# Weight pieces of a two-layer encoder: their high and low parts kept in DRAM after the first use

## The chip, the cores and the metric

The kernel runs on one core of one Trainium2 chip. The metric is device microseconds for one execution. Three runs of the kernel before gave 2173.24, 2174.95 and 2166.95 us; the median is 2173.24 us.

## The reference

Two groups of rows, `prompt` (1024 tokens, "p" below) and `sample` (512 tokens, "s"), go through the same two layers with the same weights. Cut to what matters here:

```
for l in (0, 1):
    h   = rms_norm(x, norm_g[l])
    u   = h @ w_in[l]                    # 1024 -> 15 chunks of 256 columns
    mk, mv = split(rms_norm(mem) @ w_mem_kv[l])
    l = 0: y1 = short_conv(gb, gc, hc);  y2 = window_attention(q, k, v, sink)
    l = 1: y1 = dense_gqa(q, k, v);      y2 = diff_attention(dq, dk, dv)
    ym  = memory_attention(mq, mk, mv)
    x   = x + (concat(y1, y2, ym) * silu(z)) @ w_out[l]     # 1280 -> 1024
```

`trunk(x_prompt, ...)` and `trunk(x_sample, ...)` are both computed, in float32. So every column chunk of `w_in` and `w_out` is needed by p and again by s.

## The kernel before, in words

TensorE multiplies operands of the type fp32r, which hold less than float32. Each float32 operand is therefore split: the high part is a copy rounded to fp32r, the low part is the source minus the high part. A product is three matmuls: high by high, high by low, low by high (`mm_a` lines 309 to 311, `mm_b` lines 323 to 325).

**Weights.** A chunk is 256 columns of a weight matrix. It comes in pieces of [128, 512] float32, 256 KB each: 4 pieces for `w_in` and `w_mem_kv`, 5 for `w_out`. `load_w` (line 204) does for each piece: a DMA of the raw piece into the ring `wraw` (3 slots), the high part by ScalarE into the ring `whi` (7 slots, line 186), the low part by VectorE where the piece's number is even and by GpSimd where it is odd, into the ring `wlo` (7 slots, line 187). A slot of `whi` or `wlo` comes free when the last matmul on the piece that held it is done; a slot of `wraw` when the low part is made. A piece is taken from DRAM and split again whenever its chunk is used: the run has 16 such pieces for `w_mem_kv`, 252 for `w_in` and 120 for `w_out`, 388 in all.

**Stages.** `in_proj` runs the chunks of a layer's input projection, `out_proj` the four chunks of the output projection for 512 tokens. In `out_proj` a chunk is four groups of 30 matmuls (one group for 128 tokens, 5 pieces x 2 halves x 3 matmuls), and two groups share a PSUM tile `po`, of which there are two. Attention (`swa`, `ax`, `diff`, `mem_attn`) is spread between the projections' products. In the profile of before the stages are, in us from the span's start:

| us | stage |
|---|---|
| 0 to 509 | p, layer 0: memory keys, input projection, attention, convolution |
| 509 to 572 | p, layer 0: `out_proj`, first half of the tokens |
| 572 to 632 | p, layer 0: `out_proj`, second half |
| 632 to 1160 | p, layer 1: memory keys, most of the input projection, attention |
| 1160 to 1506 | s, layer 0: input projection with p's last attention, and one chunk of p again |
| 1506 to 1599 | s, layer 0: `out_proj` |
| 1599 to 1940 | rest of p's layer 1 input projection, s layer 1 input projection, attention |
| 1940 to 2023, 2023 to 2104 | p, layer 1: `out_proj`, first and second half |
| 2104 to 2162 | s, layer 1: `out_proj` |

**Order of the work.** All data DMAs are issued by SyncE (SP) in one queue, in order (`dma`, line 105): a DMA whose operand isn't ready holds up those behind it. The program is written as a sequence, and a scheduler then places every instruction on its engine by a model of when its operands will be there; on an engine the placed order is fixed. `in_order` (line 46) makes the tiles of a ring take its slots in the order of the program. A DMA also waits for the one eight places back in the queue whose completion semaphore it shares.

Of the kernel before, what the change touches and what calls it, by code (L numbers as in the profile page):

```python
# [11 lines left out]
F32R = mybir.dt.float32r  # L12
# [6 lines left out]
D = 1024  # L19
KT = D // 128  # L20
HD = 64
# [24 lines left out]
def in_order(tc, chains):  # L46
    """Slots of a ring go to its tiles in the order of the program: the first writer of each tile is
    scheduled after that of the tile before it."""
    first = {}
    for n, ins in enumerate(tc.nc.cur_bb.bb.instructions):  # L50
        for o in ins.outs:
            t = getattr(o, "bass_ap", None)
            nm = t.tensor.name if t is not None else None
            if nm is not None and nm not in first:
                first[nm] = n, ins
    for tiles in chains.values():
        prev = None
        for _, ins in sorted((first[t.tensor.name] for t in tiles), key=lambda x: x[0]):
            if prev is not None and prev is not ins:
                tc.add_manual_dep(  # L60
                    ins, prev.name,
                    mybir.DependencyInfo(mybir.DependencyClass.NoSync, mybir.DependencyReason.DATA),
                    reason="ring",
                )
            prev = ins
# [3 lines left out]
def trunk_kernel(ctx: ExitStack, tc: tile.TileContext, a: dict, dbg=None):  # L69
# [8 lines left out]
    def ring(pool, shape, dt, tag, nm, stream=""):  # L78
        """a tile of a ring whose slots are taken in the order of the program (of its stream)"""
        t = pool.tile(shape, dt, tag=tag, name=nm, bufs=BUFS[tag])  # L80
        chains.setdefault((tag, stream), []).append(t)
        return t
# [26 lines left out]

    # ------------------------------------------------------------ constants  # L110
    ident_r = const.tile([128, 128], F32R, name="ident_r")
# [35 lines left out]

    # rotary tables with the gains folded in: cos * g and (signed) sin * g of the other half
    tab = {}
# [12 lines left out]

    # ------------------------------------------------------------ scratch in DRAM
    S = {}
# [18 lines left out]

    # ------------------------------------------------------------ helpers
    def split(out_hi, out_lo, src, lo_eng):
# [9 lines left out]
    def first(f):  # L195
        """what feeds the matrix products of the projections goes before the attention's work"""
        return f
        def g(*args, **kw):
            with tc.high_priority():
                return f(*args, **kw)  # L200
        return g

    @first
    def load_w(src, pairs):
        hi, lo = [], []
        for kp in pairs:
            lo_ = ring(sb, [128, 2, 256], F32R, "wlo", "wlo")
            h = ring(sb, [128, 2, 256], F32R, "whi", "whi")
            raw = ring(sb, [128, 2, 256], F32, "wraw", "wraw")
            dma(out=raw, in_=src[kp].rearrange("p (k n) -> p k n", k=2))  # L210
            split(h, lo_, raw, nc.vector if kp % 2 == 0 else nc.gpsimd)
            hi.append(h)
            lo.append(lo_)
        return hi, lo

    def rstd(out, ss, mul, add):
        """out = (ss * mul + add) ** -0.5"""
        n = ss.free_size()
        nc.vector.tensor_scalar(out=ss, in0=ss, scalar1=mul, scalar2=add, op0=ALU.mult, op1=ALU.add)  # L219
        e = mhalf[:, 0:n]  # L220
        if len(ss.shape) == 3:
            e = e.rearrange("p (a b) -> p a b", a=ss.shape[1])
        nc.gpsimd.tensor_tensor(out=out, in0=ss, in1=e, op=ALU.pow)  # L223
# [3 lines left out]
    def bg(n=1):  # L227
        """the next steps of the work that runs between the projections' products"""
        for _ in range(n):
            if BG:  # L230
                with tc.high_priority():
                    BG.pop(0)()

    def norm_steps(rows, put, banks="x"):
        """rms norm of 512 rows (4 sources of [128, D]), transposed; put(t, q, PSUM tile) takes it"""
        hh = {}
# [52 lines left out]
    def load_act(src, pairs):  # L289
        """pairs of [128, 2, 512], hi and lo, of src [128, n, 512] in DRAM"""  # L290
        out = []
# [9 lines left out]
    def mm_a(out, hs, sl, w, mid=None):  # L301
        """out[tok, cols] = act[:, sl].T @ w"""
        whi, wlo = w
# [11 lines left out]
    def mm_b(out, hs, w, csl, mid=None):  # L315
        """out[cols, tok] = w[:, csl].T @ act"""
        whi, wlo = w
# [16 lines left out]
    def stack_now():  # L334
        """the stack of the piece before"""
        while STACK:
            STACK.pop(0)()
# [9 lines left out]
    def between(keep=2):  # L347
        """one step of the work that goes between the projections' products"""
        if len(TAIL) > keep:
# [4 lines left out]
    def store_stack(t, nh, dst, h0, tok):  # L354
        """t [128, 2, nh, 64] (f32, SBUF): hi and lo, transposed, to dst[:, h0:h0+nh, tok:tok+256]"""
        for hp in range(nh // 2):
# [17 lines left out]
    def prep(ps, nh, dst, h0, tok, table=None, gain=None, query=False):  # L374
        """a q or k chunk ps [128, 2, nh, 64] (PSUM): rms norm (and a query's HD ** -0.5), gain, rotation"""
        raw = bw("raw")[:, 0:2 * nh * HD].rearrange("p (t h d) -> p t h d", t=2, h=nh)
# [38 lines left out]
    def put_v(ps, nh, d, dst, t0, tag="stk"):  # L415
        """ps [128, 2, nh, d] (PSUM) to dst[:, 0:nh, t0:t0+2, 0:2d], hi | lo"""
        n = min(nh, 128 // d)
# [9 lines left out]
    def silu2(ps, nm):  # L427
        """2 * silu of ps [128, 512]: ps * (1 + tanh(ps / 2))"""
        th = bw(nm)
# [3 lines left out]

    # ------------------------------------------------------------ input projection
    def rows_of(src, hf=0):
# [8 lines left out]
    def in_proj(g, l, hs, ids, ahead=None, hfs=None):  # L444
        """hfs: the halves of the tokens (all of them if not given)"""
        T = GROUPS[g]
        hfs = range(T // 512) if hfs is None else hfs
        nt = T // 128
        for ci in ids:
            kind, i = CHUNKS[l][ci]  # L450
            if ahead and ci == ids[-1]:
                ahead()
            w = load_w(a["w_in"][l, ci], range(4))
            if kind in ("z", "gch", "gbz"):
# [62 lines left out]
    def conv_cols(g, c, inner):  # L517
        """0.5 * conv along the tokens of inner; the halves follow one another"""
        n = len(inner)
# [23 lines left out]

    # ------------------------------------------------------------ memory keys and values
    def mem_rows():
# [20 lines left out]

    # ------------------------------------------------------------ attention
    def load_q(src, shape):
        """src(rows) -> AP of 64 rows; the hi rows twice and the lo rows twice"""
        out = []  # L570
# [19 lines left out]
    def fold(o, nm):  # L590
        """rows 64..127 of o [128, n] brought to rows 0..63, SBUF"""
        n = o.free_size()
# [4 lines left out]
    def finish_gqa(g, l, o, c0, tok):  # L597
        """o [128, 4, 128]: 4 heads of 128 queries; gated into y's column tiles c0, c0 + 1"""
        zg = aw("zg")[:, 0:256].rearrange("p (c t) -> p c t", c=2)
# [73 lines left out]
    def softmax(s, e, su, nm):  # L673
        """s [128, n, w] (PSUM): nm [128, n] = -max, e [128, n, w] = exp(s + nm), su [128, n] the sums"""
        nc.vector.tensor_reduce(out=nm, in_=s, axis=AXL.X, op=ALU.max, negate=True)  # L675
# [5 lines left out]
    def head_softmax(q2, k, T, e):  # L681
        """one head, 128 queries: e [128, T]: exp(scores - max), with the max of each 512 columns;
        the result [128, T / 512]: what each 512 columns are to be multiplied by"""
        n = T // 512
# [144 lines left out]
    def mem_attn(g, l, half=None, ys=None):  # L829
        """ys: hi and lo of the gated columns, where they stay on chip (512 tokens)"""  # L830
        T = GROUPS[g]
# [44 lines left out]

    # ------------------------------------------------------------ output projection
    Y_ORDER = {("p", 0): (2, 3, 4, 0, 1), ("s", 0): (2, 3, 0, 1, 4), ("p", 1): range(5), ("s", 1): range(5)}
# [4 lines left out]
    def out_proj(g, l, hf, ys, ahead=None):  # L883
# [3 lines left out]
        for ci in range(4):  # L887
            if ahead and ci == 3:
                ahead()
            w = load_w(a["w_out"][l, ci], Y_ORDER[g, l])  # L890
            for tp in range(2):
# [10 lines left out]

    # ------------------------------------------------------------ program
    nxt = {}

    def ahead(key, load):
        """before a phase ends: what it left of the background's work, and the next phase's operands"""
        def f():
# [92 lines left out]

# [1 line left out]
def host_arrays(inputs):  # L1003
# [29 lines left out]
    def pieces(w, idx):  # L1033
        # [K, 256] -> [K / 256, 128, 2 * 256]
        k = w.shape[0]
# [71 lines left out]
```

## Time and profile before

| | |
|---|---|
| median of three runs | 2173.24 us |
| span of the profiled execution, first to last instruction | 2165.8 us |
| TensorE (PE) busy | 2080.9 us, 96% |
| VectorE (DVE), ScalarE (ACT), GpSimd (POOL) busy | 71%, 55%, 50% |
| DMA | 363.74 MB, mean 168 GB/s |

The profile shows no time of its own for the profiled execution beside the span. The median of the runs is 7.4 us above the span, which is what lies around the span together with the spread of the runs (8.0 us from the lowest to the highest). PE is the engine with nearly no idle time, 84.9 us in all. Its busy time is made of overlapping matmuls, so the rate is read from the distance of their starts, not from the length of one. Means by line hide differences between stages, and so the rows below are taken by stage.

### The profile page before, as it was taken

Reading aid. Unit: us, or ns where it says so; the run is one execution under the profiler, and the core shown is the slowest. Engines: PE = TensorE matmul, PEld = TensorE weight load, DVE = VectorE, ACT = ScalarE, POOL = GpSimd, SP = SyncE. Lnnn points to the kernel's source line nnn. Section 1 sums busy time; section 2 is a strip of 40 time slices with the busy share of each in tenths; the row PEclk is TensorE's granted clock in tenths of the full one; section 3 lists DMA queues with packets and bytes.
Section 4 is the critical chain, followed back from the end, with each engine's and each line's share of the span. In section 5 each row is a group of like instructions: output and inputs, shape, how many; then the busy total and the mean of one; then the engine's idle time right before and its main releaser. Section 6 shows DMA issues by size and latency. Waiting matters only on the chain. (4 is left out here: it accounts for less than half of the span.)

```text
span 2165.8 us, 41192 instructions
## 1 busy us (share of the span) xinstructions
PE 2080.9 (96%) x14336; PEld 1916.8 (88%) x14336; DVE 1547.2 (71%) x3264; ACT 1189.7 (55%) x2838; POOL 1075.9 (50%) x1134
## 2 busy tenths in 40 slices
PE   6999999999999999999999989997998999999999
PEld 6988978889999999999998878886997899998999
DVE  8768877745445687877988886777778877875652
ACT  5545633453334566766766655546466666764441
POOL 6845532342225674853855574332346686842331
PEclk9999999999999999999999999998999999999999
DMA  6675463436776522443345565447475566567753
GB/s 229 193 214 169 140 210 106 115 100 212 250 234 220 174 84 88 131 129 114 94 121 180 165 194 166 122 147 229 143 213 179 167 186 203 175 204 217 227 169 105
DMA packets 317408, 363.74 MB, mean 168 GB/s; under 512 B 25360, under 2 KB 222736, under 8 KB 317200
## 3 DMA queue, kind: packets, MB, share of 16 engines
q1 hardware_dynamic: 317200, 361.10, 54.6%
q8 instruction: 114, 1.87, 0.4%
q14 instruction: 94, 0.77, 0.1%
HBM read 261.38 MB, written 99.61 MB: 167 GB/s over the span
## 5 line engine op out<-in xcount | busy, mean ns | idle before, releaser
L187 POOL TENSOR_TENSOR wlo<-wraw,whi 128x512 fp32r<-128x512 f32 x182 | 249.3, 1371 | 322.9 <-ACT whi L186 285.0
L186 ACT CAST whi<-wraw 128x512 fp32r<-128x512 f32 x388 | 237.3, 621 | 254.8 <-PE po L311 74.9
L677 ACT ACTIVATE e<-s,nm 128x512 f32<-128x512 f32 (+1 forms) x416 | 264.4, 640 | 173.4 <-DVE nm L675 124.5
L675 DVE TENSOR_REDUCE nm<-s 128x1 f32<-128x512 f32 (+1 forms) x368 | 248.0, 681 | 37.7 <-PE s L580 36.2
L587 DVE TENSOR_TENSOR ptlo<-pT,pthi 128x512 fp32r<-128x512 f32 x352 | 238.0, 683 | 42.6 <-ACT pthi L586 40.9
L586 ACT CAST pthi<-pT 128x512 fp32r<-128x512 f32 x352 | 201.1, 588 | 118.1 <-PE pT L665 48.4
L309 PE MATMUL po<-whi,ahi 128*128 128x256 f32 x896 | 254.7, 285 | 1.7 <-DVE xr L900 1.4
L310 PE MATMUL po<-wlo,ahi 128*128 128x256 f32 x896 | 254.0, 284 | 0.0
L311 PE MATMUL po<-whi,alo 128*128 128x256 f32 x896 | 253.5, 284 | 0.5 <-DVE alo L187 0.4
L187 DVE TENSOR_TENSOR wlo<-wraw,whi 128x512 fp32r<-128x512 f32 x206 | 175.9, 855 | 105.1 <-ACT whi L186 104.4
L309 PE MATMUL pa<-whi,ahi 128*128 128x256 f32 x768 | 221.2, 288 | 4.0 <-DVE z L431 2.1
L311 PE MATMUL pa<-whi,alo 128*128 128x256 f32 x768 | 221.3, 288 | 0.0
L310 PE MATMUL pa<-wlo,ahi 128*128 128x256 f32 x768 | 221.2, 288 | 0.0
L223 POOL TENSOR_TENSOR rs<-ss,mhalf 128x8 f32<-128x8 f32 (+2 forms) x108 | 141.7, 1313 | 149.7 <-DVE ss L219 141.6
L579 PE MATMUL s<-k,qhh 128*128 128x512 f32 (+2 forms) x512 | 194.6, 385 | 17.2 <-ACT e L677 10.6
L580 PE MATMUL s<-k,qll 128*128 128x512 f32 (+2 forms) x512 | 185.5, 367 | 2.6 <-DMA qll<-st_p1dq 1.6
L309 PEld LDWEIGHTS po<-whi,ahi 128*128 128x128 f32 x896 | 171.1, 191 | 3.7 <-DVE xr L900 1.8
L311 PEld LDWEIGHTS po<-whi,alo 128*128 128x128 f32 x896 | 171.1, 191 | 2.0 <-DVE alo L187 0.9
L310 PEld LDWEIGHTS po<-wlo,ahi 128*128 128x128 f32 x896 | 171.3, 191 | 1.3
L324 PE MATMUL pb<-h,whi 128*128 128x512 f32 x432 | 171.6, 397 | 0.0
L325 PE MATMUL pb<-h,wlo 128*128 128x512 f32 x432 | 171.4, 397 | 0.0
L323 PE MATMUL pb<-h,whi 128*128 128x512 f32 x432 | 170.9, 396 | 0.0
(171 smaller groups left out, 6272.9 us busy)
## 6 DMA issues: line engine op xcount, KB each, us to landing
wraw<-in_w_in_dram SPq DMA_DIRECT2D x252, 256.0 KB, 3.1
wraw<-in_w_out_dram SPq DMA_DIRECT2D x120, 256.0 KB, 3.4
alo<-y_p SPq DMA_DIRECT2D x20, 512.0 KB, 5.0
zg_p<-z SPq DMA_DIRECT2D x32, 256.0 KB, 3.0
k<-st_p1dk SPq DMA_DIRECT2D x14, 512.0 KB, 4.4
v<-dv_p SPq DMA_DIRECT2D x14, 512.0 KB, 5.4
zg<-zg_p SPq DMA_DIRECT2D x48, 128.0 KB, 2.7
y_p<-yo SPq DMA_DIRECT2D x48, 128.0 KB, 2.6
```

Source lines behind the costliest of these rows:

```text
L186: nc.scalar.copy(out=out_hi, in_=src)
L187: lo_eng.tensor_tensor(out=out_lo, in0=src, in1=f32(out_hi), op=ALU.subtract)
L309: nc.tensor.matmul(out=out, lhsT=h, rhs=wh, start=(k == 0), stop=False)
L310: nc.tensor.matmul(out=out, lhsT=h, rhs=wl, start=False, stop=False)
L311: nc.tensor.matmul(out=out, lhsT=l_, rhs=wh, start=False, stop=(k == n - 1))
L324: nc.tensor.matmul(out=out, lhsT=wh, rhs=l_, start=False, stop=False)
L579: nc.tensor.matmul(out=out, lhsT=q2[0], rhs=k, start=True, stop=False)
L580: nc.tensor.matmul(out=out, lhsT=q2[1], rhs=k, start=False, stop=True)
L586: nc.scalar.copy(out=hi, in_=ps)
L587: nc.vector.tensor_tensor(out=lo, in0=ps, in1=f32(hi), op=ALU.subtract)
L675: nc.vector.tensor_reduce(out=nm, in_=s, axis=AXL.X, op=ALU.max, negate=True)
L677: nc.scalar.activation(out=e[:, j, :], in_=s[:, j, :], func=ACTF.Exp, bias=nm[:, j:j + 1], accum_out=su[:, j:j + 1],)
```

## The change

`load_w` gets a key for the chunk. The first time a piece is used, its two parts are stored to two DRAM tiles of 256 KB each after they are made; every later use loads the two parts into `whi` and `wlo` and neither loads the raw piece nor splits. `w_mem_kv`, whose pieces are used once, gets no key.

```diff
-    def load_w(src, pairs):
+    def load_w(src, pairs, key=None):
         hi, lo = [], []
         for kp in pairs:
             lo_ = ring(sb, [128, 2, 256], F32R, "wlo", "wlo")
             h = ring(sb, [128, 2, 256], F32R, "whi", "whi")
+            kept = KEPT.get((key, kp))
+            if kept:
+                dma(out=h, in_=kept[0].rearrange("p (k n) -> p k n", k=2))
+                dma(out=lo_, in_=kept[1].rearrange("p (k n) -> p k n", k=2))
+                hi.append(h)
+                lo.append(lo_)
+                continue
             raw = ring(sb, [128, 2, 256], F32, "wraw", "wraw")
             dma(out=raw, in_=src[kp].rearrange("p (k n) -> p k n", k=2))
             split(h, lo_, raw, nc.vector if kp % 2 == 0 else nc.gpsimd)
+            if key:
+                both = KEPT[key, kp] = [
+                    dr.tile([128, 512], F32R, name=f"w{nm}_{key[0]}{key[1]}_{key[2]}_{kp}") for nm in "hl"
+                ]
+                for x, y in zip(both, (h, lo_)):
+                    dma(out=x.rearrange("p (k n) -> p k n", k=2), in_=y)
             hi.append(h)
             lo.append(lo_)
         return hi, lo
...
-            w = load_w(a["w_in"][l, ci], range(4))
+            w = load_w(a["w_in"][l, ci], range(4), ("i", l, ci))
...
-            w = load_w(a["w_out"][l, ci], Y_ORDER[g, l])
+            w = load_w(a["w_out"][l, ci], Y_ORDER[g, l], ("o", l, ci))
```

The rest of the diff takes out comments and moves line numbers by 16 (lines 309 to 311 become 325 to 327).

The scheduler places the new DMAs among the old ones. On SP, in the first output projection (p, layer 0, first half of the tokens), the queue of before reads as follows. `wraw` is a raw piece, `xr` the residual rows that are loaded, `x_p<-xr` the result that is stored.

```order
L106 DMA x_p<-xr 128x2x256
L106 DMA xr<-in_x_p_dram 128x2x256
L106 DMA wraw<-in_w_out_dram 128x512
L106 DMA xr<-in_x_p_dram 128x2x256
L106 DMA wraw<-in_w_out_dram 128x512
L106 DMA x_p<-xr 128x2x256
L106 DMA wraw<-in_w_out_dram 128x512 x2
```

The same place in the changed kernel; `wh_o_...` and `wl_o_...` are the DRAM tiles of the high and the low part, by chunk and piece:

```order
L106 DMA x_p<-xr 128x2x256
L106 DMA wh_o_2_2_6759<-whi 128x512
L106 DMA xr<-in_x_p_dram 128x2x256
L106 DMA wl_o_2_2_6760<-wlo 128x512
L106 DMA wraw<-in_w_out_dram 128x512
L106 DMA wh_o_2_3_6769<-whi 128x512
L106 DMA wh_o_2_4_6779<-whi 128x512
L106 DMA wl_o_2_3_6770<-wlo 128x512
L106 DMA wl_o_2_4_6780<-wlo 128x512
L106 DMA wraw<-in_w_out_dram 128x512 x2
```

Between the raw pieces stand two stores for each, which wait in the queue for the parts to be made.

On PE, at the change from the third to the last chunk of the last output projection (s, layer 1), the products of before go through one accumulator, `po_28662`, piece by piece (`whi_28639`, `whi_28645`, `whi_28651` are three pieces that follow one another):

```order
L311 MATMUL po_28662<-whi_28639,alo_27971 128x256
L309 MATMUL po_28662<-whi_28645,ahi_27979 128x256
L310 MATMUL po_28662<-wlo_28644,ahi_27979 128x256
L311 MATMUL po_28662<-whi_28645,alo_27978 128x256
L309 MATMUL po_28662<-whi_28645,ahi_27979 128x256
L310 MATMUL po_28662<-wlo_28644,ahi_27979 128x256
L311 MATMUL po_28662<-whi_28645,alo_27978 128x256
L309 MATMUL po_28662<-whi_28651,ahi_27986 128x256
```

In the changed kernel there are two accumulators, `po_28878` and `po_28943`, at that place; `whi_28867` is the third piece of the chunk and `whi_28871` the fourth:

```order
L327 MATMUL po_28878<-whi_28867,alo_28244 128x256
L325 MATMUL po_28943<-whi_28859,ahi_28231 128x256
L326 MATMUL po_28943<-wlo_28858,ahi_28231 128x256
L325 MATMUL po_28878<-whi_28871,ahi_28252 128x256
L327 MATMUL po_28943<-whi_28859,alo_28230 128x256
L325 MATMUL po_28943<-whi_28859,ahi_28231 128x256
L326 MATMUL po_28943<-wlo_28858,ahi_28231 128x256
```

The order now leaves the first accumulator after the third piece, starts the second one on pieces that are there, and comes back to the first as the fourth piece is expected.

On SP at the same place, before, three raw pieces go out together between two results:

```order
L106 DMA xr<-x_s 128x2x256
L106 DMA wraw<-in_w_out_dram 128x512
L106 DMA out_dram<-xr 128x2x256
L106 DMA wraw<-in_w_out_dram 128x512 x3
L106 DMA out_dram<-xr 128x2x256
L106 DMA wraw<-in_w_out_dram 128x512 x2
L106 DMA out_dram<-xr 128x2x256 x4
```

And in the changed kernel:

```order
L106 DMA out_dram<-xr 128x2x256
L106 DMA wlo<-wl_o_3_2_27627 128x512
L106 DMA whi<-wh_o_3_2_27626 128x512
L106 DMA whi<-wh_o_3_3_27636 128x512
L106 DMA wlo<-wl_o_3_3_27637 128x512
L106 DMA whi<-wh_o_3_4_27646 128x512
L106 DMA wlo<-wl_o_3_4_27647 128x512
L106 DMA out_dram<-xr 128x2x256 x3
```

Six loads stand where there were up to three, and each of them needs a slot of `whi` or `wlo` that PE has left, where a raw piece needed only a slot of `wraw`.

## Rows read from the trace of the kernel before

**Rows 1.** The page, part 1: busy time, share of the span, instructions.
```profile
PE 2080.9 (96%) x14336; PEld 1916.8 (88%) x14336; DVE 1547.2 (71%) x3264; ACT 1189.7 (55%) x2838; POOL 1075.9 (50%) x1134
```

**Rows 2.** Waits of PE, whole span: waiter, releaser: us in total, times, longest.
```profile
PE s L579 <- ACT e L677: 10.6, 11, 2.4
...
PE pm L309 <- ACT whi L186: 3.5, 1, 3.5
...
PE pm L310 <- DVE wlo L187: 2.0, 1, 2.0
...
PE pa L310 <- POOL wlo L187: 1.4, 1, 1.4
```

**Rows 3.** The page, part 5: groups, busy us, mean ns of one, idle before.
```profile
L187 POOL TENSOR_TENSOR wlo<-wraw,whi 128x512 fp32r<-128x512 f32 x182 | 249.3, 1371 | 322.9 <-ACT whi L186 285.0
L186 ACT CAST whi<-wraw 128x512 fp32r<-128x512 f32 x388 | 237.3, 621 | 254.8 <-PE po L311 74.9
...
L187 DVE TENSOR_TENSOR wlo<-wraw,whi 128x512 fp32r<-128x512 f32 x206 | 175.9, 855 | 105.1 <-ACT whi L186 104.4
```

**Rows 4.** The page, parts 3 and 6: DMA queue, and issues with us to landing.
```profile
q1 hardware_dynamic: 317200, 361.10, 54.6%
...
wraw<-in_w_in_dram SPq DMA_DIRECT2D x252, 256.0 KB, 3.1
wraw<-in_w_out_dram SPq DMA_DIRECT2D x120, 256.0 KB, 3.4
```

**Rows 5.** Busy time by stage; after the engines PEclk, DMA share, GB/s.
```profile
0.00:509.00 509.00, 480.81 (x2855) 422.89 (x2856) 365.77 (x783) 249.32 (x613) 239.21 (x250) 0.99 0.54 165
509.00:572.00 63.00, 62.62 (x521) 62.34 (x519) 25.36 (x35) 21.50 (x39) 14.93 (x12) 1.00 0.64 210
572.00:632.00 60.00, 57.31 (x479) 56.90 (x477) 26.83 (x41) 18.65 (x33) 11.95 (x10) 1.00 0.77 248
664.00:1160.00 496.00, 492.98 (x3638) 464.93 (x3636) 383.40 (x849) 322.67 (x768) 306.26 (x344) 1.00 0.43 133
1160.00:1470.00 310.00, 297.69 (x1763) 262.26 (x1764) 245.92 (x566) 173.11 (x423) 151.84 (x142) 0.98 0.51 155
1470.00:1506.00 36.00, 25.83 (x122) 19.78 (x121) 24.62 (x60) 21.05 (x67) 9.54 (x19) 0.81 0.89 248
1506.00:1599.00 93.00, 89.93 (x686) 85.15 (x685) 73.56 (x182) 50.73 (x128) 30.05 (x32) 1.00 0.52 153
1599.00:1940.00 341.00, 329.69 (x2318) 303.42 (x2317) 264.81 (x517) 226.54 (x547) 238.28 (x251) 0.98 0.62 188
1940.00:2023.00 83.00, 78.78 (x632) 76.59 (x631) 47.55 (x94) 35.88 (x80) 23.91 (x25) 1.00 0.76 224
2023.00:2104.00 81.00, 78.37 (x635) 76.49 (x634) 47.24 (x81) 40.07 (x94) 26.17 (x33) 1.00 0.65 199
2104.00:2162.00 58.00, 58.00 (x485) 57.79 (x483) 17.17 (x23) 10.87 (x18) 8.26 (x6) 1.00 0.39 119
580.00:600.00 20.00, 18.98 (x161) 18.78 (x160) 11.18 (x18) 7.38 (x13) 3.11 (x3) 1.00 1.07 374
640.00:650.00 10.00, 7.54 (x62) 7.03 (x61) 6.89 (x12) 7.50 (x14) 3.92 (x4) 1.00 1.03 341
```

**Rows 6.** PE in order of time, two products in the first output projection.
```profile
559.75 0.28 PE L309 MATMUL po<-whi,ahi 128*128 128x256 f32 x1
559.87 0.28 PE L310 MATMUL po<-wlo,ahi 128*128 128x256 f32 x1
```

**Rows 7.** The tile wraw, 2104 to 2162 us: ns min/median/max; landing us.
```profile
L106 SPq DMA_DIRECT2D wraw<-in_w_out_dram x13: 327/328/371, 2104.1 to 2138.0; - x13
L187 DVE TENSOR_TENSOR wlo<-wraw,whi x10: 683/693/1223, 2102.9 to 2146.9; 128x512 fp32r<-128x512 f32 x10
...
DMA to landing us min/median/max: 2.6/2.9/4.3
```

**Rows 8.** The tile wraw, 509 to 632 us, the same columns.
```profile
L106 SPq DMA_DIRECT2D wraw<-in_w_out_dram x34: 327/340/1185, 510.1 to 608.6; - x34
...
DMA to landing us min/median/max: 2.5/3.9/5.7
```

More of the change, by code (lines that the diff above doesn't have):

```diff
@@ L201, in first @@
         return g
+    KEPT = {}
     @first
-    def load_w(src, pairs):
+    def load_w(src, pairs, key=None):
         hi, lo = [], []
```

## Prediction

> **What bounds the kernel now.** I read the page's busy shares first. PE is busy 96% of the span and idle 84.9 us (2165.8 - 2080.9); DVE, ACT and POOL stand at 71, 55 and 50% [rows 1]. So a gain has to come out of those 84.9 us, and what the change takes off the other three engines counts only where PE waits for them. The second view is the list of PE's own waits: on parts of weights PE waited three times in the whole run, 3.5, 2.0 and 1.4 us [rows 2]. All three are products of the memory projection (`pm`) or first input projections (`pa` on a POOL part once), and the largest wait of another kind is 10.6 us for ACT's exponentials [rows 2]. The splitting itself is thus hidden; what it does to time is to keep ACT, DVE and POOL from attention. The third view is busy time by stage, where the reader is to see two things: PE has no idle time in the output projection of 509 to 572 us and 2104 to 2162 us and 3.0 us in 664 to 1160 us, while 1160 to 1940 us, where attention sets the pace in places, has 12.3 + 10.2 + 3.1 + 11.3 = 36.9 us; and the DMA engines, at 54.6% over the run [rows 4], are far above that in the output projections, up to 1.07 of full with 374 GB/s in 580 to 600 us [rows 5].
>
> **The change part by part.** Of 388 pieces 16 have no key. First uses are 30 chunks x 4 pieces of `w_in` and 8 x 5 of `w_out`, 160; later uses are 252 - 120 = 132 and 120 - 40 = 80, 212.
>
> *Removed:* 212 casts of 0.621 us on ACT, 131.7 us; for the 132 later `w_in` pieces the low parts go half to DVE and half to POOL, for `w_out` three of five are even, so 66 + 48 = 114 on DVE of 0.855 us, 97.5 us, and 66 + 32 = 98 on POOL of 1.371 us, 134.4 us [rows 3]. And 212 raw loads of 256 KB. Nothing of it is on PE, which does the same matmuls.
>
> *Added:* 320 stores and 424 loads of parts in place of 212 raw loads, a net 532 DMAs of 0.262 MB, 139.5 MB on top of 361.1 MB [rows 4]. The question is where these 139.5 MB fall, and what the queue of SP holds up. By stage:
>
> A. First output projection, 509 to 572 us. Before, 210 GB/s x 63 us = 13.2 MB [rows 5]. Forty stores add 10.5 MB: 23.7 MB. The two busiest stretches moved 374 and 341 GB/s with the DMA engines full [rows 5]; at these 23.7 MB takes 63.4 or 69.5 us where 63 are there. That is a loss of 0.4 to 6.5 us. I take 6: bytes come in bursts behind waits in the queue, and the slower row is the mixed one. The matmuls stand 0.12 us apart here [rows 6] with nothing else on PE to fill in, so a late piece is lost time.
>
> The Trainium skill, page "DMA: Bandwidth & Descriptors", section Specifications, puts the memory's share of one core at about 358 GB/s, and its section Measured has 425 GB/s for a core alone with very large transfers. By the first, A is estimated at 3.2 us, by the second at nothing. The trace's 374 GB/s at a full share is between them and nearer the first.
>
> B. Second half, 572 to 632 us. 248 x 60 = 14.9 MB, and 20 pieces of net one extra load add 5.2 MB: 20.1 MB, 54 to 59 us at the two rates, so there is room on average. But 580 to 600 us ran full already, and PE was busy 18.98 of those 20 us [rows 5]. Of the five pieces of a chunk and the two ahead, 7 extra parts or 1.8 MB land in it, 5 us at 374 GB/s. Bounds 0 and 5, taken 4.
>
> C. First half of p's layer 1 output projection, 1940 to 2023 us. 224 x 83 = 18.6 MB, and 40 stores make it 29.1 MB: 77.8 or 85.3 us. Bounds 0 and 8 (the 2.3 us of the slower rate, and about as much again as B's burst), taken 4, since attention of s is mixed in and gives PE other work.
>
> D. Chunk changes on loaded parts. The slot of a new chunk's third piece comes free after 6 of the last group's 30 products and the piece is wanted after 24 + 12 more: 36 x 0.12 = 4.3 us [rows 6]. Before, within that time came only a cast and a subtraction (0.62 + 0.69 or 1.37 us) of a piece that had landed; now come the issue and flight of two DMAs. At the quiet end that is 0.33 + 0.33 + 2.9 = 3.6 us [rows 7], which fits; with the flight of 509 to 632 us it is 0.34 + 0.34 + 3.9 = 4.6 us, 0.3 late, and with the longest, 0.7 + 5.7 = 6.4 us, 2.1 late [rows 8]. The new order on PE goes over to the second accumulator at this place, which covers some of it. There are 12 such changes in dense stretches (second half of p in both layers, and s, layer 1). Bounds 0 and 12 x 2.1 = 25, taken 12 x 0.4 = 5. What is queued behind such a load on SP is the store of a result, the residual rows and the next parts; DVE's addition waits for the rows, and the accumulator for DVE.
>
> E. The input projections with stores, 0 to 509 and 664 to 1160 us: 240 stores, 62.9 MB, make 165 and 133 GB/s into about 228 and 196 [rows 5], below full. Each store waits on SP for the low part, and behind it stand raw loads and attention's operands. The cover is the three raw slots. Bounds 0 and 8, taken 2; the nearest row is PE's 3.0 us of idle time in 664 to 1160 us, which shows a stage with much slack in its queues.
>
> F. Relief in 1160 to 1940 us. 152 of the 212 later pieces lie here (132 of `w_in`, 20 of `w_out`): 94 us of ACT's 471, 78 x 0.855 = 67 us of DVE's 609, 74 x 1.371 = 101 us of POOL's 430 [rows 3, 5]. PE is idle 36.9 us here. Bounds 0 and -36.9. I take a third, -12: the idle time hangs on chains of attention in which the splits are one of many neighbours on engines that are 55 to 78% busy.
>
> G. The loads of the same stretch: 152 x 0.262 = 39.8 MB in 780 us, 51 GB/s on top of 153 to 248 [rows 5]. In 1470 to 1506 us the DMA engines stand at 0.89 and PE at a mean granted clock of 0.81, part of it at the 1.2 GHz level, after idle time [rows 5]; the operands of attention and the first parts for the next output projection meet there. Bounds 0 and 12 (10.2 us are idle now), taken 4.
>
> Sum: 6 + 4 + 4 + 5 + 2 - 12 + 4 = 13. The span goes from 2165.8 to 2178.8 us; with the 7.4 us by which the median of the runs stands above the span, 2186 us. Lower ends together are -36.5 us, upper ends 64.5.
>
> **The rivals.** *Absorbed (0.25).* DMA engines are fast enough: the stores lag behind harmlessly, the second accumulator hides the late pieces, and A to E and G come to some 10 us against relief of 10. For it speaks that A's deficit is 0.4 us at the best rate, against it that three stretches come to 0.9 of full or more: 2173 us.
>
> *Relief decides (0.22), faster.* The mechanism is attention's chain in 1160 to 1940 us: PE waits for ACT's exponentials, ACT's queue has a cast of 0.62 us in between, DVE a subtraction that takes 0.855 in the mean and 0.69 us in a quiet stretch [rows 3, 7]. If three quarters of the 36.9 us come back, -28, and costs stay at 6, the time is 2173 - 22 = 2151. It decides as soon as what comes back exceeds the costs by 11 us. For it speaks that ACT ends PE's largest waits; against it that 664 to 1160 us, with the same kinds of work and all splits in place, has PE at 99%.
>
> The Trainium skill, page "SBUF — State Buffer", section Who interferes with whom, says that a DVE instruction with two SBUF inputs contends with a GpSimd instruction that reads SBUF. By that rule each POOL subtraction that goes also frees DVE's neighbours, which favours this rival; the spread of DVE's subtraction, 683 to 1223 ns [rows 7], agrees with it.
>
> *The queue of SP decides (0.15).* 2085 instead of 1553 DMAs go through one queue in order, and loads that wait for PE stand before attention's operands. Issue alone is no bound (2085 x 0.34 = 709 us), but the longest issue was 1.2 us with the engines full [rows 8], and D at 20, G at 10 and E at 8 without F's full relief (-10) make A to G come to 42: 2215 us.
>
> That the change doesn't do what it says is no rival: the order has 212 pairs of loads in place of raw pieces.
>
> **How the numbers follow.** The forecast of 2186 us has 0.38, with a range of its own from 2174 to 2202. About 0.5% (11 us) is what a measurement can tell from no change. Of the forecast 0.32 lies above 2184 and 0.06 within; absorbed lies within, relief is faster, SP's queue slower: 0.22 faster, 0.31 same, 0.47 slower. For 8 in 10 the range goes from 2150, which takes in most of relief, to 2220, the middle of SP's case and more.
>
> **What would show it.** DMA share near 1 and PE idle by some 6 us in the first output projection; PE waits that name `whi<-wh_o` or `wlo<-wl_o` at chunk changes of the last 160 us, together 3 to 9 us; PE idle in 1160 to 1940 us down from 36.9 to about 29; ACT at about 1058, DVE 1450 and POOL 942 us busy. The prediction is wrong if the output projections keep their 62, 60 and 222 us, or if the idle time in the attention stretches goes down by more than half, or if chunk changes cost 1 us or more each.

## The result, and the profile after

The changed kernel takes 2183.68 us (median of four runs, 2180.6 to 2184.99) beside 2170.09 us of the kernel before on the same chip (2166.32 to 2174.95): a ratio of 1.0064, with a 95% interval of 1.0041 to 1.0086. It is slower, by about 14 us, where 13 were forecast. The profiled execution took 2184.99 us with a span of 2183.1 us.

The page after, part 1, the DMA queue, two of the groups and four of the kinds of issues (columns as in [rows 1, 3, 4]):

```profile
PE 2096.0 (96%) x14336; PEld 1922.9 (88%) x14336; DVE 1438.8 (66%) x3150; ACT 1076.8 (49%) x2626; POOL 931.9 (43%) x1036
...
q1 hardware_dynamic: 393808, 500.59, 71.0%
...
L187 POOL TENSOR_TENSOR wlo<-wraw,whi 128x512 fp32r<-128x512 f32 x84 | 115.5, 1376 | 171.7 <-ACT whi L186 105.4
...
L186 ACT CAST whi<-wraw 128x512 fp32r<-128x512 f32 x176 | 107.8, 621 | 135.0 <-PE po L327 33.9
...
wraw<-in_w_in_dram SPq DMA_DIRECT2D x120, 256.0 KB, 4.0
...
wl_i<-wlo SPq DMA_DIRECT2D x120, 256.0 KB, 3.2
whi<-wh_o SPq DMA_DIRECT2D x80, 256.0 KB, 5.0
wlo<-wl_o SPq DMA_DIRECT2D x80, 256.0 KB, 5.2
```

The reader is to see that the change did what it says: 388 casts have become 176, ACT is 113 us less busy, DVE 108 and POOL 144, and the queue moves 139.5 MB more. PE has the same 14336 matmuls, and its idle time only went from 84.9 to 87.1 us: of the 17.3 us by which the profiled span is longer, 15.1 are longer busy time for the same matmuls. A raw piece lands in 4.0 us where it took 3.1, a loaded part of `w_out` in 5.0 to 5.2.

The stages, cut near the places where PE reaches the same work; the counts of products in brackets show how far the cuts agree with those of before (us, busy of PE, PEld, DVE, ACT, POOL with counts, PEclk, DMA share, GB/s); compare [rows 5]:

```profile
0.00:511.00 511.00, 483.50 (x2854) 424.39 (x2855) 367.27 (x783) 249.12 (x613) 237.60 (x250) 0.98 0.70 228
511.00:574.00 63.00, 61.05 (x500) 60.12 (x500) 19.91 (x29) 15.61 (x28) 10.42 (x8) 1.00 0.97 340
574.00:647.00 73.00, 65.84 (x497) 63.99 (x496) 21.25 (x36) 12.61 (x22) 4.98 (x6) 0.91 0.82 277
647.00:690.00 43.00, 35.99 (x278) 34.33 (x277) 29.16 (x44) 22.25 (x43) 19.18 (x18) 0.92 0.93 309
690.00:1184.00 494.00, 489.12 (x3591) 460.05 (x3591) 372.29 (x828) 315.23 (x748) 302.79 (x338) 1.00 0.57 185
1184.00:1470.00 286.00, 285.04 (x1718) 252.03 (x1717) 205.50 (x523) 134.21 (x349) 101.66 (x106) 1.00 0.73 235
1470.00:1530.00 60.00, 43.52 (x208) 31.98 (x206) 42.30 (x104) 35.80 (x100) 12.46 (x21) 0.86 0.76 208
1530.00:1615.00 85.00, 84.51 (x661) 81.37 (x662) 58.82 (x156) 37.24 (x104) 22.50 (x31) 1.00 0.67 205
1615.00:1957.60 342.60, 331.40 (x2327) 304.20 (x2327) 234.11 (x492) 194.97 (x481) 184.68 (x214) 0.99 0.77 241
1957.60:2041.50 83.90, 81.75 (x651) 78.98 (x650) 49.87 (x97) 35.67 (x83) 24.81 (x25) 1.00 1.03 335
2041.50:2120.50 79.00, 76.18 (x593) 73.93 (x593) 30.86 (x55) 22.98 (x59) 10.84 (x20) 0.96 0.75 244
2120.50:2179.00 58.50, 57.92 (x482) 57.51 (x480) 6.83 (x10) 1.14 (x2) 0.00 (x0) 1.00 0.65 219
```

Four things stand in it. From 511 to 690 us the DMA engines are at 0.82 to 0.97 of full, and the second half of the output projection (574 to 647 us) and the stage behind it (647 to 690) have 14 us of PE idle time, where before 572 to 632 us had 2.7 [rows 5] and the stage behind it 3.1:

```profile
632.00:664.00 32.00, 28.91 (x228) 28.20 (x227) 24.22 (x40) 19.30 (x39) 15.47 (x14) 0.95 0.82 271
```

PE is also busy for longer there: 65.84 us for 497 products in the second half, where 57.31 us were enough for 479 [rows 5], at a mean granted clock of 0.91 instead of 1.00. From 1184 to 1470 us PE has 1 us of idle time, where before it had 12.3 in 1160 to 1470 [rows 5]. And the last three output projections take 83.9, 79.0 and 58.5 us beside 83, 81 and 58 [rows 5], even with the engines at 1.03 in the first.

What PE waits for in 511 to 706 us of the changed kernel (waiter, releaser: total, times, longest):

```profile
PE hT L269 <- DVE ht L280: 8.0, 7, 1.8
PE po L326 <- DMA x_p<-xr: 3.7, 1, 3.7
PE hT L269 <- DVE ss L235: 1.3, 1, 1.3
```

The first row of the same view of before, in 509 to 690 us, is

```profile
PE hT L253 <- DVE ht L264: 4.1, 3, 1.8
```

The long wait is a low part that came late. The releaser is given as a store; the operand is `wlo`, as the row of that product in order of time shows (in brackets the idle time before it). The weight load ahead of it waited 3.9 us for the DMA `wlo<-wl_o`, which SP had issued 8.4 us before the product started:

```profile
572.09 0.42 SPq L106 DMA_DIRECT2D wlo<-wl_o  x1
```

```profile
580.53 0.38 PE L326 MATMUL po<-wlo,ahi 128*128 128x256 f32 x1 [3.74 <-DMA x_p<-xr]
```

The other loads of that stretch were slow too. In 560 to 606 us the low parts landed like this in the changed kernel (min, median, max in us):

```profile
L106 SPq DMA_DIRECT2D wlo<-wl_o x12: 319/423/1056, 560.4 to 603.6; - x12
...
DMA to landing us min/median/max: 3.9/5.4/9.1
```

The rows of the residual that the next normalization reads (`x`, 512 KB) landed like this, after and then before:

```profile
L106 SPq DMA_DIRECT2D x<-x_p x4: 319/351/423, 571.2 to 584.8; - x4
...
DMA to landing us min/median/max: 6.1/6.7/8.2
```

```profile
L106 SPq DMA_DIRECT2D x<-x_p x4: 326/379/496, 563.5 to 576.4; - x4
...
DMA to landing us min/median/max: 3.2/4.0/6.2
```

So it is not only the weights that come late there: the normalization's rows do too, and its transposes (`hT`) are where PE then waits most, 8.0 us beside 4.1, each time for DVE to take over an earlier one. That these waits come from the late rows is likely and not shown.

PE also ran slower around these waits. From 581.8 to 588.6 us, just behind the wait of 3.74 us, and again from 598.8 to 605.6 us the granted clock is at its 1.2 GHz level, and 572 to 605 us has 0.80 in the mean:

```profile
572.00:605.00 33.00, 26.14 (x170) 24.49 (x170) 14.97 (x26) 9.16 (x16) 2.20 (x4) 0.80 0.97 336
```

At that level products start 0.21 us apart, where [rows 6] has 0.12 us:

```profile
585.24 0.41 PE L327 MATMUL po<-whi,alo 128*128 128x256 f32 x1
585.45 0.41 PE L325 MATMUL po<-whi,ahi 128*128 128x256 f32 x1
```

Of what the second half lost, 4.5 us are idle time (7.2 beside 2.7), and some 6 are longer busy time (65.84 us less 497 times the 0.12 us of before). Over the run the mean clock went from 0.988 to 0.983. By an estimate from these two means and the two distances, PE spent some 22 us more at the lower level, which is some 10 of its 15.1 us of longer busy time.

### The profile page after: what moved, and what is told of

Read it like the earlier page. It is cut to its first block, busy times and chain, and to the rows that moved or that the text cites. A ratio compares the mean times of both kernels' runs of the same rounds, so it can differ in the third digit from the quotient of the medians.

```text
span 2183.1 us, 41403 instructions
## 1 busy us (share of the span) xinstructions
PE 2096.0 (96%) x14336; PEld 1922.9 (88%) x14336; DVE 1438.8 (66%) x3150; ACT 1076.8 (49%) x2626; POOL 931.9 (43%) x1036
## 4 chain that ended last, share of the span: by engine, by line
PE 76%; DMA 11%; DVE 5%; issue 2%; ACT 2%; POOL 2%; SPq 1%; ACTq 0%; DVEq 0%; POOLq 0%
PE pb L339 7%; PE pb L340 7%; PE pb L341 7%; PE pa L325 6%; PE pa L326 6%; PE pa L327 6%; PE s L595 4%; PE s L596 4%; PE po L326 4%; PE po L327 4%; PE po L325 4%; PE o L751 3%; PE pT L747 3%; PE stT L382 1%; DMA wraw<-in_w_in_dram 1%
## 5 line engine op out<-in xcount | busy, mean ns | idle before, releaser
L187 POOL TENSOR_TENSOR wlo<-wraw,whi 128x512 fp32r<-128x512 f32 x84 | 115.5, 1376 | 171.7 <-ACT whi L186 105.4
L186 ACT CAST whi<-wraw 128x512 fp32r<-128x512 f32 x176 | 107.8, 621 | 135.0 <-PE po L327 33.9
L326 PE MATMUL pa<-wlo,h 128*128 128x256 f32 x576 | 164.8, 286 | 1.4 <-POOL wlo L187 1.4
```

Source lines behind the costliest of these rows:

```text
L326: nc.tensor.matmul(out=out, lhsT=h, rhs=wl, start=False, stop=False)
```

## The experiments

All eleven kernels were timed in five rounds beside the kernel before, whose median was 2166.93 us beside e1 to e4, 2167.72 beside e5 to e8 and 2168.01 beside e9 to e11. The ratios are estimated over all rounds and differ from the quotient of two medians by up to 0.14%. To see where time goes, I compared the start of the n-th matmul of PE, counted over all matmuls, with its start before. The table gives the difference in us at ten places of the profiled executions (the columns are the numbers of the experiments, "chg" the changed kernel):

```
matmul  before   chg   e1    e2    e3    e4    e5    e6    e7    e8    e9   e10   e11
 2800    496.8  +2.1  +3.5  -2.2  +0.6  -1.7  -1.0  -2.5  -0.3  -1.0  +1.7  +4.5  -0.4
 3200    551.4  +4.4  +3.8  +1.1  +4.4  -2.3  -0.5  -3.1  -0.5  -0.8  +3.3  +4.3  -1.0
 3600    602.1 +14.8  +3.3  +6.3  +9.7  +1.9  +7.8  -3.1  -1.0  -1.3  +3.1  +5.0  -2.3
 4000    655.2 +20.5  +3.8  +9.2  +8.8  +5.9 +12.6  -3.3  -0.6  -1.4  +4.7  +3.4  -3.9
 4400    706.6 +22.7  +9.3  +5.1 +14.7  +3.5 +15.7  +2.6  -1.5  -2.0  +4.3  +9.3  -3.9
 7600   1140.3 +25.0 +11.8  +5.7 +16.6  +3.2 +20.1  +5.6  -0.2  -1.9  +4.9 +11.7  -3.4
 9200   1418.3  +8.1  -6.8  +9.2 +18.3  -8.8  +1.7  +5.2  +4.4  +2.1  -9.4  -7.2 -15.0
 9600   1507.5 +13.5  +0.8 +12.9 +22.0 -10.4  +7.9  +8.8 +11.7  +3.7 -11.2  -4.9 -15.9
12800   1967.8 +14.1  +5.8 +27.7 +34.3  -5.4 +12.9 +12.5 +14.4 +12.5  -9.6  -2.6  -7.4
14335   2161.7 +17.2  +1.4 +30.9 +34.3  -2.6 +19.0  +9.2 +11.3 +11.1  -8.7  -3.4  -6.6
```

Differences of some 3 us stand there already at the first place, also in kernels whose work is that of before up to it (e6 and e2, -2.5 and -2.2); smaller steps are not read. Further on single executions come apart by more: from matmul 4400 to 12000 e1 and e10 have the same order on PE and the same loads and stores, and yet they go from 0.4 to 5.7 us apart between 9200 and 9600. A single step below some 6 us shows nothing by itself.

**e1, only w_in kept.**

```diff
-            w = load_w(a["w_out"][l, ci], Y_ORDER[g, l], ("o", l, ci))
+            w = load_w(a["w_out"][l, ci], Y_ORDER[g, l])
```

> Only the pieces of w_in are kept (w_out goes back to raw loads and splits). Theory 1 (the cost is DMA traffic of w_out's parts in and right after p's first output projection, some 20 us between 511 and 690 us; the gain is relief of ACT, DVE and POOL in the attention stretches): the 20 us go and the relief stays, 2160 to 2170 us, not slower than before. Rival (the queue of SP: cost by number of DMAs): 240 stores and 132 extra loads, 372 of the 532 added DMAs, are still there, so about 0.7 of the loss, 2179 us.

Measured: 2164.88 beside 2166.93 us, 0.9984 (0.9969 to 0.9999). As theory 1 had it; the count of DMAs alone would have given 2179. In the table the 16 us that the changed kernel lost between matmuls 3200 and 4000 are gone; 5.5 us are still lost just behind, between 4000 and 4400, where layer 1's first chunks are stored.

**e2, only w_out kept.**

```diff
-            w = load_w(a["w_in"][l, ci], range(4), ("i", l, ci))
+            w = load_w(a["w_in"][l, ci], range(4))
```

> Only the pieces of w_out are kept. Theory 1: the cost of 511 to 690 us stays and most of the relief goes, so it is as slow as the changed kernel or slower, 2182 to 2195 us. Rival (number of DMAs): 160 of the 532 added DMAs, 0.3 of the loss, 2174 us.

Measured: 2199.32 us, 1.0148 (1.0128 to 1.0169), slower than either theory. Only 7 us are lost by matmul 4400; 22 us come between 7600 and 12800, where only 20 pieces are loaded in parts and, at the very end, eight stored. Theory 1 had no step for that, so the next runs were chosen for it too.

**e3, stores without loads.**

```diff
-            if kept:
+            if False:
...
-            if key:
+            if key and not kept:
```

> All 320 stores of first uses are made, but nothing loads them: later uses load the raw piece and split it, as before. Theory 1: the stores' share of 511 to 690 us (some 10 us) and no relief, 2176 to 2184 us; the stretch from 1184 us on is as in the kernel before. Rival (number of DMAs): 320 of 532, 2178 us, with the loss spread over all stages that store.

Measured: 2201.93 us, 1.0152 (1.013 to 1.0174), a miss for both. By matmul 4400 it has lost 14.7 us, the stores' share. From 7600 to 12800 it loses another 18, all of it between its last store of `w_in` (1188 us) and its first store of layer 1's `w_out` (1966 us), where it neither stores nor loads a part: the work is that of the kernel before.

**e4, loads without stores.**

```diff
             if key:
-                both = KEPT[key, kp] = [
...
+                KEPT[key, kp] = SOME[kp]
+            elif len(SOME) < 8:
+                both = [dr.tile([128, 512], F32R, name=f"w{nm}_some_{len(SOME)}") for nm in "hl"]
+                SOME.append(both)
```

> Later uses load two parts without a split, but first uses store nothing; the parts loaded are those of eight pieces of w_mem_kv that are stored at the start, so the numbers are not those of the weights. Theory 1: relief of the attention stretches (-16 us before 1470 us) and the loads' share of p's second half (some 8 us) and of 1470 to 1530 us (some 10 us): 2168 to 2178 us. Rival (number of DMAs): 212 extra loads and 16 stores, 0.43 of the loss, 2176 us.

Measured: 2161.53 us, 0.9968 (0.9952 to 0.9984), better than expected. The loads lose 5 us by matmul 4400, against 14 of the stores in e3; the two make up most of the 20.6 us of the changed kernel from 2800 to 4400. From 7600 to 9600 it gains 13.6.

**e5, both parts in one tile and one DMA of 512 KB.**

```diff
-            lo_ = ring(sb, [128, 2, 256], F32R, "wlo", "wlo")
-            h = ring(sb, [128, 2, 256], F32R, "whi", "whi")
+            hl = ring(sb, [128, 2, 2, 256], F32R, "whl", "whl")
+            h, lo_ = hl[:, 0], hl[:, 1]
...
-                dma(out=h, in_=kept[0].rearrange("p (k n) -> p k n", k=2))
-                dma(out=lo_, in_=kept[1].rearrange("p (k n) -> p k n", k=2))
+                dma(out=hl, in_=kept.rearrange("p (a k n) -> p a k n", a=2, k=2))
```

> The changed kernel with both parts of a piece in one tile, stored and loaded by one DMA of 512 KB: the same bytes, 160 net DMAs more than before instead of 532. If bytes are what costs: 2176 to 2192 us, the output projection of 511 to 690 us as long as in the changed kernel. If the number of DMAs in SP's queue is what costs: 0.3 of the loss, about 2170 us.

Measured: 2192.0 beside 2167.72 us, 1.0102 (1.0083 to 1.012). The bytes are the same:

```profile
q1 hardware_dynamic: 340240, 500.57, 69.4%
```

With 372 DMAs fewer the loss by matmul 4400 is still 15.7 us, and the time is at the upper end of what was expected if bytes cost. The number of entries in SP's queue is not what costs most of it.

**e6, only layer 1's w_in kept.**

```diff
-            w = load_w(a["w_in"][l, ci], range(4), ("i", l, ci))
+            w = load_w(a["w_in"][l, ci], range(4), ("i", l, ci) if l else None)
```

with `w_out` as in e1.

> Only the pieces of layer 1's w_in are kept. Theory 1 (traffic where the DMA engines are full costs, relief gains): as with all of w_in, without the 2 to 6 us that the first 511 us lose there: 2158 to 2168 us. If relief is the sum of all removed splits, 72 of 132 pieces remain and the gain over w_out's loss is halved: 2172 us.

Measured: 2178.32 us, 1.0047 (1.003 to 1.0064), a miss. It loses 6 us by its stores between 4000 and 4400, nothing moves between 7600 and 9200, and 7 are lost up to 12800. So relief doesn't go with the number of splits removed: the 72 later pieces of layer 1 bring nothing that shows. Its order on PE is another one than that of before, so a smaller relief could be hidden in what the order costs.

**e7 and e8, a single piece kept.** Here the work is that of before to within 1 MB, but the scheduler places another order.

```diff
-            if key:
+            if key == ("i", 1, 3) and kp == 0:
```

and for e8 `key == ("i", 1, 13) and kp == 0`.

> One single piece of the 160 is kept (layer 1, w_in, fourth chunk, first piece): 2 stores and a few loads more, about 1 MB, under 2 us of work; but the scheduler's order on PE differs from before in most of the attention stretches from 700 us on. Theory 2 (the order that the scheduler happens to place is worth up to 1% in the stretch of 1170 to 1960 us, and made up the 20 us that the stores-only kernel lost there with no added work): the time differs from before by 8 us or more, either way. Rival (added transfers are what costs there too): within 4 us of before.

> One other single piece is kept (layer 1, w_in, fourteenth chunk, first piece): the order on PE is that of before up to about 1090 us and another one after it. Theory 2: equal to before up to 1090 us, then apart by 8 us or more, either way. Rival: within 4 us of before throughout.

Measured: e7 2178.99 us, 1.0052 (1.0036 to 1.0068); e8 2180.09 us, 1.0056 (1.004 to 1.0072). e7 moves this much:

```profile
q1 hardware_dynamic: 317632, 361.89, 54.0%
```

At the 340 GB/s measured above, 0.8 MB more than before are 2.3 us, not 11. Both follow before to matmul 7600 within 2 us and then lose 14 by 12800. In e7 12 of these come between 7600 and 9600 (1140 to 1519 us), and its two stores (716 to 718 us) and two loads (1707 us) lie outside that stretch. The placed order by itself is worth 0.5% in these two. What it does can be seen where 800 products of PE take 123 us before and 130 in e7; DVE, ACT and POOL do nearly the same work in it. PE is idle for 8.3 us instead of 5.7, and busy for 121.70 instead of 117.30 at a mean granted clock of 0.96 instead of 0.99. Before, then e7, then the changed kernel for the same products:

```profile
1212.00:1335.00 123.00, 117.30 (x803) 107.69 (x802) 100.96 (x227) 71.68 (x177) 79.63 (x76) 0.99 0.53 160
```

```profile
1211.00:1341.00 130.00, 121.70 (x800) 110.07 (x799) 105.18 (x230) 73.63 (x178) 82.21 (x77) 0.96 0.53 159
```

```profile
1228.00:1345.00 117.00, 117.00 (x803) 107.59 (x803) 89.48 (x225) 60.74 (x157) 61.21 (x66) 1.00 0.74 237
```

The changed kernel's PE has no idle time at all there, with ACT, DVE and POOL at 61, 89 and 61 us. In e8 the largest wait of PE in 1140 to 1530 us is one that before had for 5.2 us; the 9 us that e8 loses behind matmul 9600 were not traced to a wait:

```profile
PE s L595 <- ACT e L693: 11.3, 8, 5.8
```

**e9, only layer 0's w_in kept.**

```diff
-            w = load_w(a["w_in"][l, ci], range(4), ("i", l, ci))
+            w = load_w(a["w_in"][l, ci], range(4), ("i", l, ci) if l == 0 else None)
```

with `w_out` as in e1.

> Only layer 0's w_in is kept: 60 pieces stored in the first 511 us, where the DMA engines have room, and loaded by s layer 0 in 1160 to 1506 us. The order on PE is that of before from about 1570 us on. If relief is real and sits where s layer 0 loads its parts, the loss of 511 to 706 us is gone, and the late stretch is as before: about 2 lost, 10 to 16 gained, 2152 to 2163 us, faster than both kernels. If the gain seen at 1140 to 1420 us in the changed kernel was only another order, or relief is nothing: 2166 to 2178 us.

Measured: 2157.94 beside 2168.01 us, 0.994 (0.9919 to 0.9962). It beats both kernels. The stores go out where there is room, and the loads take the splits out of the stretch in which p's last attention and s's layer 0 share the engines: -16 us from matmul 7600 to 9600. Behind that the order is that of before and the difference stays.

```profile
PE 2077.0 (96%) x14336; PEld 1912.6 (89%) x14336; DVE 1520.1 (70%) x3234; ACT 1159.5 (54%) x2778; POOL 1029.9 (48%) x1104
```

Sixty casts fewer do more here than 212 in the changed kernel.

**e10, the changed kernel without layer 0's w_out.**

```diff
-            w = load_w(a["w_out"][l, ci], Y_ORDER[g, l], ("o", l, ci))
+            w = load_w(a["w_out"][l, ci], Y_ORDER[g, l], ("o", l, ci) if l else None)
```

> The changed kernel without layer 0's w_out; layer 0 and 1 of w_in and layer 1's w_out are kept. Theory 1: 14 of the 20 us that the changed kernel lost between 511 and 706 us go (5 or 6 stay, the stores of layer 1's first w_in chunks), and layer 1's w_out costs next to nothing in 1958 to 2179 us (under 4 us against w_in alone): 2164 to 2172 us. Rival (w_out costs wherever it is kept, by late parts at chunk changes): 2175 to 2185 us.

Measured: 2166.15 us, 0.999 (0.9976 to 1.0005), as theory 1 had it. The 16 us between matmuls 3200 and 4000 go with layer 0's `w_out`; where that is kept alone (e2), the same stretch loses 8.1, so half of them need the other parts' traffic or the order too. Layer 1's `w_out`, stored and loaded in parts in the last 200 us, costs nothing that shows: from 12800 to the end the difference goes from -2.6 to -3.4.

**e11, e9 without the last two chunks.**

```diff
-... ("i", l, ci) if l == 0 else None)
+... ("i", l, ci) if l == 0 and ci not in (13, 14) else None)
```

> As layer 0's w_in alone, without its last two chunks: 52 of the 60 pieces. The order on PE is the same as there up to about 1480 us and another one after it, where neither kernel has any loaded part or store. Theory 2 (order): equal up to 1480 us within 3 us, then 8 us or more slower, as the two kernels with one piece kept. Rival (order is worth little): the same time within 4 us.

Measured: 2165.52 us, 0.9985 (0.9972 to 0.9998); its profiled run is its fastest, so the table shows it 4 us too good. Against e9 it gains 4.7 us up to matmul 9600 and then loses 9.3, where e9 loses 2.5, on the same work in another order. The direction and about the size are those of theory 2; the first part was 5 us apart, not within 3, so as a pair it is weaker than e7 and e8. By the medians the two are 7.6 us apart.

## Why the prediction was right

The time was forecast at 2186 and came at 2183.68 us. Where the sum said +13, the medians of the two kernels on this chip differ by 13.6 us and the two profiled spans, which the table compares, by 17.3. The steps, in us from the table:

| step | forecast | measured in the changed kernel |
|---|---|---|
| A, first output projection | +6 | +2.3 |
| B, its second half | +4 | +10.4 (matmuls 3200 to 3600) |
| none: 632 to 706 us of before | 0 | +7.9 (3600 to 4400) |
| E, stores of the input projections | +2 | +2.1 up to 497 us, +2.3 in 707 to 1140 |
| F and G, 1140 to 1968 us | -8 | -10.9 (7600 to 12800) |
| C and D in the last three output projections | +4, +5 | +3.1 in all |

Cut exactly at the first products of the two halves (matmuls 2856, 3336 and 3848), A is +2.3 and B +10.9. A, E and the last row are below the 6 us that a single step needs.

**What was right.** PE's work stayed the same, the 140 MB had to be paid where the engines were already busy, and relief came only in the attention stretches. The estimate of a full DMA engine from [rows 5] held: 63 us at 340 GB/s and 84 us at 335 GB/s were measured with shares of 0.97 and 1.03. The Trainium skill's page "DMA: Bandwidth & Descriptors", section Specifications, has about 358 GB/s for one core's share of memory, and its section Measured 425 GB/s for loads of 16 MB. The two stretches, with 256 KB transfers in both directions, lie 5 to 6% below the first and some 20% below the second; the 374 GB/s of 20 us in [rows 5] lie above the first. PE's idle time in the attention stretches, forecast to fall from 36.9 to about 29 us, came to 29.1 (1184 to 1957.6 us).

**What was mis-sized.** Step B said that on average there is room and only the burst of 580 to 600 us would come later. It measured 10.4 us, twice its upper bound of 5: near a full share the flights grew (5.4 us for a low part, 6.7 for the normalization's rows), and the normalization, which comes between the two halves, waited too. What the step left out is the clock: it priced bytes alone, and some 6 of the 10.4 us are products that ran at the 1.2 GHz level around PE's waits. The sum had no term at all for the memory keys and first chunks of layer 1 behind it, where 341 GB/s stood in [rows 5]; it cost 7.9, and e1, e6 and e10, which store layer 1's first `w_in` chunks there and have no parts of layer 0's `w_out`, lose 4.3 to 6.0 in it. Against that A was 3.7 too large: 63 us at 340 GB/s are 21.4 MB of its 23.7, so some 2 MB came later. D was too large as well: late parts at chunk changes cost PE next to nothing in the last stages (in 1957 to 2183 us),

```profile
PE po L325 <- DMA whi<-wh_o: 0.8, 2, 0.4
...
PE po L326 <- DMA wlo<-wl_o: 0.4, 2, 0.2
```

though the parts flew longer than D's 3.9 us (tile `wlo`, 2120 to 2183 us):

```profile
L106 SPq DMA_DIRECT2D wlo<-wl_o x16: 320/422/737, 2120.8 to 2164.2; - x16
...
DMA to landing us min/median/max: 2.9/4.8/6.5
```

That the change to the second accumulator, which the prediction took as a partial cover, covered nearly all of it is likely; no run went without it. In the first layer, on fuller DMA engines, one late part did cost 3.74 us (at 580.5 us), more than the 2.1 us that D had as its longest.

**What was luck.** B and the stage without a term cost 14 us more than the sum had, and A, C, D, F and G together came out 12 us better. The span was 4.3 us longer than the forecast 2178.8, and the median stands 0.6 us above it and not 7.4: the profiled execution took 1.9 us more than its span, so most of the 7.4 was spread between runs.

**What was right for another reason than given.** F and G together came out near the forecast, but they hold a third cause that no rival had. Kernels with the splits still in place (e2, e3, e7, e8) lose 14 to 22 us between 1140 and 1968 us, where the order is another one than in the kernel before; e7 and e8 show that the order alone can do it. The kernels that load layer 0's parts there (e1, e4, e5, e9, e10, e11 and the changed one) gain 12 to 19 from matmul 7600 to 9200. They do so in four different orders on PE, and the five that load none there (e2, e3, e6, e7, e8), in four others, come to between -0.4 and +4.6; so this gain is relief and not one lucky order. It is about as large as F's -12 or larger where it acts, s's layer 0, and none of it shows where the forecast counted it too, s's layer 1 (e6). In the changed kernel the gain up to 1418 us is partly given back from 1418 to 1507 (+5.4, with a mean clock of 0.86 in 1470 to 1530 us). That these 5.4 us are the order and not G's loads isn't settled: e9 has the same loads of s layer 0 and loses nothing there, but e9 doesn't load the first parts of `w_out`, and e1, which doesn't either, loses 7.6. e10, with the same order and work as e1 there, loses 2.3, so 5.4 us are within what single executions differ by.

Of the rivals, "absorbed" holds for layer 1's `w_out`; "relief decides" holds for e9, in the place that it named and at 16 of the 28 us (matmul 7600 to 9600); "the queue of SP decides" fails by its size (E came to 4.4 us and the chunk changes of the last stages to 1.2, where it needed 8 and 20) and, as far as the number of DMAs goes, by e5. Why e2 and e3 lose more (22 and 18 us) than e7 and e8 in the same stretch is open: their orders are again other ones, and no run took their order without their stores.

## What to carry to other kernels

Trading arithmetic for transfers is decided stage by stage: here the same edit gains 0.6% where the loads fall into a stretch with DMA to spare and waiting engines, and loses some 0.7% (16 us) where the added bytes take both halves of an output projection from 0.64 and 0.77 of full to 0.97 and 0.82. Look at every stage in which bytes are added, the neighbours included, since near-full engines delayed the other loads there as well as the new ones, and look at the granted clock around PE's waits. And where a scheduler places the order, measure a neutral edit as well (one piece of 160 here): a difference of its 0.5% says nothing about the idea. The changed kernel's own 0.6% is hardly more; what carries its account are the steps by stage and the runs that take single parts away.

## What the runs showed that I had not expected

A kernel with one weight piece kept, 0.8 MB in 362, was 0.52 and 0.56% slower, with intervals clear of no change. And stores alone (e3) were dearer than stores and loads together: 1.0152 beside 1.0064.
